# Two unread tiles of 64 and 480 bytes that shift the tile pools of an encoder layer

## The chip, the cores and the metric

The kernel runs on 1 core of one Trainium2 chip. The metric is the device time of one execution in microseconds (us), the median of several runs; lower is better. TensorE (PE in the profile) multiplies, VectorE (DVE) and ScalarE (ACT) work on elements, GpSimd (POOL) and SyncE (SP) mostly issue DMAs. A matmul has a moving operand, whose columns stream through the array, and a stationary operand of 128 by 128, which a separate weight load (PEld) puts in place beforehand. Both are read from SBUF, the on-chip memory, of which every one of the 128 partitions holds an equal stretch of bytes.

## The reference

One layer of an encoder over 256 tokens of width 2048, all in float32. Around every part stands an RMS norm before and one after:

```python
f = _swiglu(_rmsnorm(h, ffn1_pre_g[i]), ffn1_w_gate[i], ffn1_w_up[i], ffn1_w_down[i])
h = h + 0.5 * _rmsnorm(f, ffn1_post_g[i])
m = _mixer(_rmsnorm(h, mix_pre_g[i]), w_qkv[i], na_rpb[i], out_g[i], w_o[i])
h = h + _rmsnorm(m, mix_post_g[i])
f = _swiglu(_rmsnorm(h, ffn2_pre_g[i]), ffn2_w_gate[i], ffn2_w_up[i], ffn2_w_down[i])
h = h + 0.5 * _rmsnorm(f, ffn2_post_g[i])
g = jax.nn.sigmoid(_rmsnorm(h, ple_pre_g[i]) @ w_ple_gate[i])
h = h + _rmsnorm(g * (p[i] @ w_ple_proj[i]), ple_post_g[i])
```

`_swiglu(u)` is `(silu(u @ w_gate) * (u @ w_up)) @ w_down` with a hidden width of 5632. The mixer projects to q, k and v by one matrix of 2048 by 6144, attends in 16 heads of 128, and projects back by `w_o`, 2048 by 2048.

## The kernel before

**Products.** Every large product is made from two parts of each operand: a rounded high part and the low part that is left (`hid_h` and `hid_l`, `wh` and `wl`). `mac` (lines 92 to 106) issues three matmuls for each 128 rows of the inner dimension: high by high (L104), low by high (L105), high by low (L106). The activations, transposed, are the stationary operand, 128 columns of 4 bytes, which is 512 bytes in a partition. The weights are the moving operand, 512 columns, which is 2048 bytes. Weights come by DMA into `raw` or `raw_b`; `split` (lines 71 to 80) makes `wh` from them on ACT (L77) and `wl` on DVE (L78), two blocks of 128 rows at a time, into seven buffers each.

**Stages.** ffn1 and ffn2 go through the hidden width in 11 blocks of 512 columns (`swiglu`). The first block makes gate and up by plain products; the other ten use `pair_product`, which gets gate and up of both token tiles from seven products, as in Strassen's scheme, over 14 of the 16 row blocks. Of these seven, four have sums of activations as stationary operand (`sums_h`, `sums_l`, made by `token_sums`, L318 to L343; seven row blocks each, so 21 matmuls), three have the activations themselves (`u_h`, `u_l`); `rest` does the remaining row blocks, with `u_h` and `u_l` too. Between these, at the points named `fill()`, the down product of the block before is run in four pieces, each with `hid_h` and `hid_l` as stationary operand: 4 row blocks, 2 token tiles and 3 matmuls, 24 a piece. The last block's down product uses one tile `hid_2` for both parts (`hid` in the profile). The mixer's q, k and v use `u_h` and `u_l`; its output product (`mo`) uses the attention's output, again in tiles called `hid_h` and `hid_l`. The last stage's gate product (`pg`) uses `u_h` and `u_l`.

**Memory.** Pools stand one behind another: on the left side from low addresses up, in the order in which they are opened, and on the right side from the top down. A pool that is closed leaves its place to the next one. Where the tiles of the program before begin, as its allocation says, in bytes within a partition:

| tile | pool | start | remainder by 512 |
|---|---|---|---|
| `sums_h` | resid | 4096 | 0 |
| `u_h`, `u_l` (4 buffers each) | acts | 20480 and up, 36864 and up | 0 |
| `raw` (3), `wh` (7), `wl` (7) | wpool | 53248, 77824, 106496 and up | 0 |
| `y_s`, `y_g` and others | work | 135168, 137216 | 0 |
| `ssf`, `m`, `r` and others, 32 bytes each | small | 139264 to 140735 | any |
| `hid_h`, `hid_l`, `f`, `raw_b`, `sums_l` of ffn1, `hid_2`; the attention's `qT`, `kT`, `v`, `pts`; `pp`, `z` | those opened behind small | 140736 and up | 448 |
| `f`, then `sums_l` of ffn2 | f2 (right side, top at 229344) | 198624, 215008 | 480 |

The parts of `u_h`, `u_l` and `hid_h`, `hid_l` for one row block and one token tile are 512 bytes long, at steps of 1024 bytes from row block to row block and 512 from tile to tile; those of `sums_h` and `sums_l` follow each other at steps of 512 bytes.

**Order.** The framework plans the order of each engine's instructions when the program is built, so a few matmuls stand ahead of where the text of the kernel has them: the first four of the last `rest` of a `pair_product` run before the product of `a22` (L274 before L271). Engines wait for each other by semaphores that the framework puts in.

Of the kernel before, what the change touches and what calls it, by code (L numbers as in the profile page):

```python
# [8 lines left out]
F32 = mybir.dt.float32  # L9
# [6 lines left out]
P = 128  # L16
# [18 lines left out]
def encoder_layer(ctx: ExitStack, tc: tile.TileContext, a: dict, out: bass.AP):  # L35
# [13 lines left out]
    small = ctx.enter_context(tc.tile_pool(name="small", bufs=4))  # L49
# [2 lines left out]
    ps_o = ctx.enter_context(tc.tile_pool(name="ps_o", bufs=2, space=PSUM))  # L52


    ident = const.tile([P, P], F32, name="ident")
    make_identity(nc, ident)
    mhalf = const.tile([P, 16], F32, name="mhalf")
# [680 lines left out]
    f_pool = sums_pool[0] = ffn2.enter_context(tc.tile_pool(name="f2", bufs=1, side="right"))  # L738
# [46 lines left out]
        list(res)  # L785

    pool = ctx.enter_context(tc.tile_pool(name="ple", bufs=1))
    pp = []
    for n, pool_, tag in ((RQ, f_pool, "sums_l"), (NT * D // NB - RQ, pool, "pp")):
        y = pool_.tile([P, n, NB], F32, name="pp", tag=tag)  # L790
# [108 lines left out]
```

## Time and profile before

| | us |
|---|---|
| median of 3 runs (lowest, highest) | 1917.34 (1916.06, 1917.87) |
| the profiled execution's own time | 1919.31 |
| its span, first to last instruction | 1917.5 |
| PE, PEld, DVE, ACT, POOL busy | 1895.1, 1553.7, 1584.0, 1172.9, 217.5 |
| HBM read, written | 413.70 MB, 4.19 MB |

The profile is of one execution. A matmul's entry lasts from its start to a modelled end, some 390 ns for 512 columns, and the next one starts before that end. How fast TensorE really goes is therefore read from the starts: the distance from one matmul's start to the next one's. The timeline view prints starts in us with two digits; over a run of 21 or 24 matmuls the mean distance is known to about half a nanosecond.

### The profile page before, as it was taken

To read this page: it belongs to the slowest core of one execution; us is meant where nothing else is said; L and a number is where in the kernel's file an instruction comes from. 1 tells how busy PE (TensorE), PEld (TensorE's weight loads), DVE (VectorE), ACT (ScalarE), POOL (GpSimd) and SP (SyncE) were. 2 spreads that over 40 slices of the span, in tenths; PEclk is the share of its full clock that TensorE was granted. 3 is DMA by queue.
4 is the path that set the end of the run, shared out by engine and by line. 5 is a ranking of instruction groups with operands and counts; after the bars stand their busy time and mean duration, and the time that the engine had idled before them with its cause. 6 is when DMAs were issued, how large, how long until landed. Compare 5 with 4: busy or idle time off the path is not lost.

```text
span 1917.5 us, 23547 instructions
## 1 busy us (share of the span) xinstructions
PE 1895.1 (99%) x8546; PEld 1553.7 (81%) x8546; DVE 1584.0 (83%) x1825; ACT 1172.9 (61%) x1476; POOL 217.5 (11%) x189
## 2 busy tenths in 40 slices
PE   8999999999999999999999999999999999999997
PEld 6888888888888878888888888888888888888786
DVE  8889999989998986567565588899999899898954
ACT  7766666666666664554545466666666666665753
POOL 1110101010111000000000001101010111100100
PEclk9999999999999999999999999999999999999999
DMA  9879877897779567354454569789777977795562
GB/s 344 243 238 268 254 201 205 246 275 214 191 239 268 158 228 242 137 176 164 144 178 179 193 217 276 215 252 264 212 196 237 275 238 190 227 273 170 182 241 99
DMA packets 210533, 419.44 MB, mean 219 GB/s; under 512 B 8944, under 2 KB 12016, under 8 KB 209136
## 3 DMA queue, kind: packets, MB, share of 16 engines
q1 hardware_dynamic: 172304, 343.47, 50.7%
q0 software_dynamic: 38112, 74.46, 21.7%
q8 instruction: 67, 1.10, 0.2%
q14 instruction: 50, 0.41, 0.1%
HBM read 413.70 MB, written 4.19 MB: 218 GB/s over the span
## 4 chain that ended last, share of the span: by engine, by line
PE 91%; issue 5%; DVE 1%; ACT 1%; DMA 1%; POOL 0%; SPq 0%; POOLq 0%; DVEq 0%; ACTq 0%
PE pair_g L104 10%; PE pair_g L105 9%; PE pair_g L106 9%; PE down L104 8%; PE down L105 8%; PE down L106 8%; PE pair_u L105 4%; PE pair_u L104 4%; PE pair_u L106 4%; PE v L106 2%; PE v L104 2%; PE v L105 2%; PE tr L308 1%; PE q L104 1%; PE q L106 1%
## 5 line engine op out<-in xcount | busy, mean ns | idle before, releaser
L77 ACT CAST wh<-raw_b 128x1024 fp32r<-128x1024 f32 (+1 forms) x546 | 514.2, 950 | 296.2 <-PE down L105 158.2
L78 DVE TENSOR_TENSOR wl<-raw_b,wh 128x1024 fp32r<-128x1024 f32 (+1 forms) x546 | 582.3, 1097 | 75.9 <-ACT wh L77 69.0
L77 ACT CAST wh<-raw 128x1024 fp32r<-128x1024 f32 (+1 forms) x417 | 435.2, 1051 | 317.0 <-PE down L105 61.1
L78 DVE TENSOR_TENSOR wl<-raw,wh 128x1024 fp32r<-128x1024 f32 (+1 forms) x417 | 500.6, 1219 | 149.0 <-ACT wh L77 136.5
L191 POOL DMA_DIRECT2D raw_b<-in_ffn_w_up x156 | 180.3, 1197 | 1036.1 <-DVE wl L78 965.7
L105 PE MATMUL down<-wh,hid_l 128*128 128x512 f32 x640 | 251.8, 393 | 0.0
L104 PE MATMUL down<-wh,hid_h 128*128 128x512 f32 x640 | 251.1, 392 | 0.0
L106 PE MATMUL down<-wl,hid_h 128*128 128x512 f32 x640 | 248.7, 389 | 0.0
L106 PE MATMUL pair_g<-wl,u_h 128*128 128x512 f32 x502 | 196.1, 391 | 0.0
L104 PE MATMUL pair_g<-wh,u_h 128*128 128x512 f32 x502 | 195.9, 396 | 0.0
L105 PE MATMUL pair_g<-wh,u_l 128*128 128x512 f32 x502 | 195.6, 390 | 0.0
L199 DVE TENSOR_TENSOR raw_b<-raw_b 128x1024 f32<-128x1024 f32 (+1 forms) x156 | 164.4, 1096 | 0.1
L104 PEld LDWEIGHTS down<-wh,hid_h 128*128 128x128 f32 x640 | 120.2, 188 | 27.7
L106 PEld LDWEIGHTS down<-wl,hid_h 128*128 128x128 f32 x640 | 120.1, 188 | 27.0
L105 PEld LDWEIGHTS down<-wh,hid_l 128*128 128x128 f32 x640 | 120.3, 188 | 24.3
L469 DVE TENSOR_TENSOR f<-f,down 128x512 f32<-128x512 f32 x160 | 109.5, 684 | 9.3 <-PE down L106 5.2
L105 PE MATMUL pair_g<-wh,sums_l 128*128 128x512 f32 x288 | 113.8, 395 | 0.0
L104 PE MATMUL pair_g<-wh,sums_h 128*128 128x512 f32 x288 | 113.7, 395 | 0.0
L104 PEld LDWEIGHTS pair_g<-wh,u_h 128*128 128x128 f32 x502 | 94.2, 188 | 23.5 <-ACT u_s L206 3.8
L106 PE MATMUL pair_g<-wl,sums_h 128*128 128x512 f32 x288 | 112.3, 390 | 0.0
L106 PEld LDWEIGHTS pair_g<-wl,u_h 128*128 128x128 f32 x502 | 94.2, 188 | 20.6
L105 PEld LDWEIGHTS pair_g<-wh,u_l 128*128 128x128 f32 x502 | 94.3, 188 | 18.6
(227 smaller groups left out, 3028.6 us busy)
## 6 DMA issues: line engine op xcount, KB each, us to landing
raw<-in_ffn_w_down SPq DMA_DIRECT2D x88, 1024.0 KB, 8.1
raw_b<-in_ffn_w_up POOLq DMA_DIRECT2D x120, 512.0 KB, 10.3
raw<-in_w_qkv SPq DMA_DIRECT2D x48, 1024.0 KB, 5.1
raw_b<-in_ffn_w_gate SPq DMA_DIRECT2D x40, 1024.0 KB, 6.4
raw_b<-in_ffn_w_gate SPq DMA_DIRECT2D x36, 768.0 KB, 8.0
raw_b<-in_ffn_w_up SPq DMA_DIRECT2D x20, 1024.0 KB, 7.1
raw<-in_w_o SPq DMA_DIRECT2D x16, 1024.0 KB, 4.9
raw<-in_w_ple_gate SPq DMA_DIRECT2D x16, 1024.0 KB, 5.0
```

The source lines that it names most:

```text
L77: nc.scalar.copy(wh[:, :n], raw),
L78: nc.vector.tensor_tensor(wl[:, :n], raw, wh[:, :n].bitcast(F32), op=ALU.subtract),
L104: nc.tensor.matmul(acc, xh, wh, start=lead, stop=False, skip_group_check=True)
L105: nc.tensor.matmul(acc, xl, wh, start=False, stop=False, skip_group_check=True)
L106: nc.tensor.matmul(acc, xh, wl, start=False, stop=tail, skip_group_check=True)
L191: nc.gpsimd.dma_start(raw[:, k0:k1], weight_rows(w, j, c, k0, k1), accum_op=ALU.add)
L199: nc.vector.tensor_tensor(x[:, j], x[:, j], y[:, j], op=ALU.add)
L308: nc.tensor.transpose(tr[:, k], x[:, k * P : (k + 1) * P], ident)
L469: nc.vector.tensor_tensor(f_t, f_t, acc, op=ALU.add)
```

## The change

Two tiles are allocated that nothing writes or reads. The first, 16 columns of 4 bytes (64 bytes in a partition), is the first tile of the pool `small`. The second, 120 columns (480 bytes), is the third kind of tile of the pool `f2`, asked for after ffn2. No instruction is added, removed or moved in the kernel's text.

```diff
@@ -52,6 +52,7 @@
     ps_o = ctx.enter_context(tc.tile_pool(name="ps_o", bufs=2, space=PSUM))
 
 
+    small.tile([P, 16], F32, name="align", bufs=1)
     ident = const.tile([P, P], F32, name="ident")
     make_identity(nc, ident)
     mhalf = const.tile([P, 16], F32, name="mhalf")
@@ -785,6 +786,7 @@
         list(res)
 
     pool = ctx.enter_context(tc.tile_pool(name="ple", bufs=1))
+    f_pool.tile([P, 120], F32, name="align")
     pp = []
     for n, pool_, tag in ((RQ, f_pool, "sums_l"), (NT * D // NB - RQ, pool, "pp")):
         y = pool_.tile([P, n, NB], F32, name="pp", tag=tag)
```

## Prediction

> **What bounds the kernel now.** I read the page first, then the groups of instructions with shapes apart, then the timeline of TensorE.
>
> ```profile
> span 1917.5 us, 23547 instructions
> PE 1895.1 (99%) x8546; PEld 1553.7 (81%) x8546; DVE 1584.0 (83%) x1825; ACT 1172.9 (61%) x1476; POOL 217.5 (11%) x189
> PEclk9999999999999999999999999999999999999999
> PE 91%; issue 5%; DVE 1%; ACT 1%; DMA 1%; POOL 0%; SPq 0%; POOLq 0%; DVEq 0%; ACTq 0%
> ```
>
> TensorE is busy 99% of the span at full granted clock, and 91% of the chain of waits lies on it. What shortens the time must therefore shorten the distance between matmul starts. The groups give the number of matmuls by their stationary operand, the only operand of the large products that the change moves (`wh` and `wl` lie in a pool opened before `small`):
>
> ```profile
> L105 PE MATMUL down<-wh,hid_l 128*128 128x512 f32 x640 | 251.8, 393 | 0.0
> L105 PE MATMUL pair_g<-wh,sums_l 128*128 128x512 f32 x288 | 113.8, 395 | 0.0
> L105 PE MATMUL pair_u<-wh,sums_l 128*128 128x512 f32 x264 | 104.3, 395 | 0.0
> L105 PE MATMUL mo<-wh,hid_l 128*128 128x512 f32 x128 | 50.0, 391 | 0.0
> L105 PE MATMUL down<-wh,hid 128*128 128x512 f32 x64 | 25.0, 391 | 0.0
> L105 PEld LDWEIGHTS down<-wh,hid_l 128*128 128x128 f32 x640 | 120.3, 188 | 24.3
> L105 PEld LDWEIGHTS pair_g<-wh,u_l 128*128 128x128 f32 x502 | 94.3, 188 | 18.6
> ```
>
> A weight load takes 188 ns at either offset, and the matmuls' own durations are modelled, so the groups tell nothing of speed. The starts do. Here is the first matmul of each run in one stretch of ffn2, and of one run of the last stage:
>
> ```profile
> 1304.53 0.39 PE L104 MATMUL pair_u<-wh,u_h 128*128 128x512 f32 x1
> ...
> 1307.25 0.40 PE L104 MATMUL pair_u<-wh,sums_h 128*128 128x512 f32 x1
> ...
> 1312.10 0.40 PE L104 MATMUL pair_g<-wh,sums_h 128*128 128x512 f32 x1
> ...
> 1316.95 0.39 PE L104 MATMUL down<-wh,hid_h 128*128 128x512 f32 x1
> ...
> 1322.45 0.40 PE L104 MATMUL pair_g<-wh,sums_h 128*128 128x512 f32 x1
> ...
> 1863.75 0.39 PE L104 MATMUL pg<-wh,u_h 128*128 128x512 f32 x1
> ...
> 1869.19 0.39 PE L104 MATMUL pg<-wh,u_h 128*128 128x512 f32 x1
> ...
> 1874.63 0.39 PE L104 MATMUL pg<-wh,u_h 128*128 128x512 f32 x1
> ```
>
> With `u_h`, `u_l` (both at remainder 0 by 512) 12 matmuls take 2.72 us and 24 take 5.44 us twice, once for each token tile: 226.7 ns each. With `hid_h`, `hid_l` (both at 448) 24 take 5.50 us, 229.2 ns each. With `sums_h` (0) and `sums_l` (480) 21 take 4.85 us twice, 231.0 ns each. All these are back to back, with no idle time in their groups, the same clock, the same moving buffers. In ffn1, where `sums_l` is at 448:
>
> ```profile
> 279.71 0.39 PE L104 MATMUL down<-wh,hid_h 128*128 128x512 f32 x1
> ...
> 285.20 0.39 PE L104 MATMUL pair_g<-wh,sums_h 128*128 128x512 f32 x1
> ...
> 285.89 0.40 PE L104 MATMUL pair_g<-wh,sums_h 128*128 128x512 f32 x1
> ...
> 286.61 0.40 PE L104 MATMUL pair_g<-wh,sums_h 128*128 128x512 f32 x1
> ...
> 290.06 0.39 PE L104 MATMUL pair_g<-wh,u_h 128*128 128x512 f32 x1
> ```
>
> The down run takes 5.49 us, 228.8 ns a matmul, and the 21 with sums 4.86 us, 231.4 ns. Within these the first triple takes 0.69 us and the second 0.72, where `u` has 0.68 (2.72 for four). So the distance follows the low part of the stationary operand's address; a change of 32 bytes in it (448 to 480) leaves the mean and slightly changes its pattern.
>
> **The change part by part.** The first tile adds 64 bytes to `small`. Everything behind it moves from 140736 to 140800, which is 275 times 512: remainder 448 becomes 0. The second adds 480 bytes to a pool that hangs from the top, so its base goes down: `f` from 198624 to 198144 (387 times 512) and `sums_l` from 215008 to 214528 (419 times 512). No instruction, wait or DMA is added. I price each operand that becomes aligned by the distance that the aligned `u` has, 226.7 ns; this is the one step which the trace shows only for other tiles.
>
> - Sums: 3 times (288 + 264) = 1656 matmuls, now (231.0 + 231.4) / 2 = 231.2 ns: 4.5 ns less each is -7.5 us.
> - Down pieces: 3 times 640 = 1920, now (229.2 + 228.8) / 2 = 229.0: 2.3 ns each is -4.4 us.
> - The mixer's output product, 3 times 128 = 384, and the last down products, 3 times 64 = 192:
>
> ```profile
> 1060.82 0.39 PE L104 MATMUL mo<-wh,hid_h 128*128 128x512 f32 x1
> ...
> 1066.31 0.39 PE L104 MATMUL mo<-wh,hid_h 128*128 128x512 f32 x1
> ...
> 1785.69 0.39 PE L104 MATMUL down<-wh,hid 128*128 128x512 f32 x1
> ...
> 1796.68 0.39 PE L104 MATMUL down<-wh,hid 128*128 128x512 f32 x1
> ```
>
> 24 in 5.49 us and 48 in 10.99 us, so 228.8 and 229.0; 2.1 and 2.3 ns each make -0.8 and -0.4 us.
>
> What does not come through. After the third sums product (`s3`) TensorE may go on in that bank only when ACT has copied it, and four matmuls of `rest` fill that time:
>
> ```profile
> PEld pair_g L104 <- ACT u_s L206: 3.8, 18, 0.2
> L78 DVE TENSOR_TENSOR wl<-raw_b,wh 128x1024 fp32r<-128x1024 f32 x420 | 502.0, 1221 | 74.5 <-ACT wh L77 67.6
> L78 DVE TENSOR_TENSOR wl<-raw,wh 128x1024 fp32r<-128x1024 f32 x415 | 499.2, 1222 | 148.3 <-ACT wh L77 135.8 <-PE mo L106 1.5
> L77 ACT CAST wh<-raw_b 128x1024 fp32r<-128x1024 f32 x420 | 437.8, 1050 | 264.1 <-PE down L105 158.2 <-PE pair_u L105 52.7 <-PE pair_g L105 23.8
> L77 ACT CAST wh<-raw 128x1024 fp32r<-128x1024 f32 x415 | 433.9, 1053 | 316.3 <-PE down L105 61.1 <-PE pair_g L105 42.0 <-PE k L105 39.6
> 287.95 1.05 ACT L77 CAST wh<-raw 128x1024 fp32r<-128x1024 f32 x1 [0.76 <-PE pair_g L105]
> 289.04 1.23 DVE L78 TENSOR_TENSOR wl<-raw,wh 128x1024 fp32r<-128x1024 f32 x1 [0.59 <-ACT wh L77]
> 290.53 0.39 PE L106 MATMUL pair_g<-wl,u_h 128*128 128x512 f32 x1
> ```
>
> TensorE already waits there 18 times. Those four take 4 times some 5 ns less, and the wait grows by that: 18 times 0.02 is +0.4 us. The elementwise work does not change: the split of an operand at 448 (`raw_b`) takes 1221 ns on DVE and 1050 on ACT, at 0 (`raw`) 1222 and 1053, so I take zero, with bounds of 420 times 3 ns, 1.3 us, to either side, hidden as long as DVE stays ahead. The tightest place is the last three rows: ACT starts at 287.95, when TensorE has let a buffer go, DVE's `wl` ends at 290.27 and is used at 290.53, 0.26 us later. Between 287.95 and 290.53 TensorE gains 11 matmuls times 4.5 ns, 0.05 us, so the cover holds; were it gone, each 0.1 us of lateness would cost 20 blocks times 0.1, 2 us. The small products of the attention have aligned operands after the change as well. Their sum is
>
> ```profile
> L668 PE MATMUL o<-v,pts 128*128 128x128 f32 x128 | 18.4, 287 | 0.0
> L645 PE MATMUL sc<-kT_h,qT_h 128*128 128x256 f32 x32 | 10.0, 312 | 0.0
> ```
>
> 128 and three groups of 32, 224 matmuls; by the largest mean step seen above, 4.5 ns, they give between -1.0 and +1.0 us, and I take 0, the middle.
>
> Sum: -7.5 - 4.4 - 0.8 - 0.4 + 0.4 = -12.7 us. The span of 1917.5 becomes 1904.8 and the profiled execution's 1919.3 becomes 1906.6. That execution lies 2.0 us above the median of 1917.34, so the median is forecast at 1904.6 us.
>
> **The rivals.**
>
> 1. *Only one of the two groups gains.* The hid and sums tiles lie above 140000 bytes and the `u` tiles below 53248, so a high address could be the cause instead of the remainder. Against it: in both, distances vary by place in the triple (0.69 and 0.72 us), which a fixed price of a far read would not do. If only the sums gain: -7.5 + 0.4, 1910 us. If only the hid tiles gain, because `sums_h` and `sums_l` stand 200 KB apart: -5.6, 1912 us.
>
> 2. *No effect.* The distances belong to what runs beside the matmuls, DVE and ACT above all, and the stretches with `u` in the last stage have less of that. Against it: the 12 matmuls with `u` at 1304.53, between down and sums in ffn2, run at 226.7 too. Or an unread tile is dropped from the allocation, and the change does nothing. 1917.3 us either way. The Trainium skill says in "SBUF — State Buffer", section "Who interferes with whom", that PE and ACT never wait on anyone, and in its section "Operand start alignment" it asks of a start address only a multiple of the element size (for legality; it says nothing on speed). By the first of these the change would give nothing. The trace disagrees so far: 226.7, 229.0 and 231.2 ns for the same work.
>
> 3. *Slower: the sums collide at every step.* What counts may be the stationary operand's place against the moving stream, and sums aligned in both parts at steps of 512 bytes are a combination that no row shows. If each triple then ran like the worst in ffn1 (285.89 to 286.61, 0.72 us against 3 times 231.2, 0.694), 552 triples times 0.026 are +14.4 us; with the others' -5.2 the end is 1926.5 us. It is slower than before once a triple of sums exceeds 0.694 + 5.2 / 552 = 0.703 us. Against it: the `u` of the second token tile starts 512 bytes beyond that of the first, and the runs from 1863.75 and from 1869.19 both have 226.7.
>
> 4. *The second tile misses.* If it is laid elsewhere in its pool, `sums_l` of ffn2 stays at 480, half of the 7.5 us is lost, 1908.4 us.
>
> **How the numbers follow.** Chances: forecast 0.66; rival 1, 0.13; rival 4, 0.05; rival 2, 0.09; rival 3, 0.07. The forecast's own range: if aligned runs settle less well than `u` there remain some 0.6 ns on 4152 matmuls, 2.5 us, and with the bounds above, 1.0 and 1.3, about 1909; on the other side, the `u` runs that follow sums gain as well. There the run
>
> ```profile
> 97.09 0.40 PE L104 MATMUL pair_g<-wh,u_h 128*128 128x512 f32 x1
> ...
> 110.73 0.39 PE L104 MATMUL down<-wh,hid_h 128*128 128x512 f32 x1
> ```
>
> takes 13.64 us for 60, 227.3 ns, 0.6 more than elsewhere; over some 2000 matmuls with `u` in the pairs 1.2 us, with the same 1.0 and 1.3, about 1901. With rivals 1 and 4 the range is 1900 to 1915 us, which leaves out rivals 2 and 3, 0.16, and a little of the rest. A change of this kernel can be told from none beyond 0.2%, 3.8 us. Faster: forecast, rival 1 and rival 4, less a little, 0.83. Same: rival 2 and a little, 0.10. Slower: 0.07.
>
> **What would show it.** In the profile after: down runs of 24 at 5.44 us and sums runs of 21 at 4.76 us; `u` unchanged at 226.7; the same counts of instructions; DVE and ACT durations of the splits within 3 ns; the wait of PEld for ACT's `u_s` longer by some 0.02 us each. I am wrong if a run with aligned stationary operands keeps 229 or 231 ns, if a triple of sums goes beyond 0.70 us, or if matmul starts are evenly 226.7 ns and the gain turns up as waits for `wl`.

## The result and the profile after

The changed kernel takes 1904.53 us (median of 6 runs, 1902.86 to 1905.71) against 1917.52 us before on the same chip: a ratio of 0.9932 with a 95% interval of 0.9919 to 0.9944, 13.0 us faster. The forecast was 1904.6 us for the changed kernel. The profiled execution has its own time of 1905.38 us and a span of 1903.6 us.

These are the first lines of the profile after, and its chain of waits by engine:

```profile
span 1903.6 us, 23547 instructions
...
PE 1880.1 (99%) x8546; PEld 1551.1 (81%) x8546; DVE 1580.4 (83%) x1825; ACT 1174.5 (62%) x1476; POOL 217.5 (11%) x189
...
PE 91%; issue 5%; DVE 1%; ACT 1%; DMA 1%; POOL 0%; SPq 0%; POOLq 0%; DVEq 0%; ACTq 0%
```

The numbers of instructions are those of before on every engine, and so are the shares of the chain: TensorE is busy for the same share of a span that is 14 us shorter. Where the time went shows in the timeline of TensorE. Here is the first matmul of each run in the same stretch of ffn2 (all source lines stand one or two further on, since the change puts in lines; the first matmul of `mac` is now L105), and of one stretch of ffn1:

```profile
1295.10 0.39 PE L105 MATMUL pair_u<-wh,u_h 128*128 128x512 f32 x1
...
1297.82 0.39 PE L105 MATMUL pair_u<-wh,sums_h 128*128 128x512 f32 x1
...
1302.58 0.39 PE L105 MATMUL pair_g<-wh,sums_h 128*128 128x512 f32 x1
...
1307.34 0.39 PE L105 MATMUL down<-wh,hid_h 128*128 128x512 f32 x1
...
1312.78 0.39 PE L105 MATMUL pair_g<-wh,sums_h 128*128 128x512 f32 x1
...
277.78 0.39 PE L105 MATMUL down<-wh,hid_h 128*128 128x512 f32 x1
...
283.22 0.39 PE L105 MATMUL pair_g<-wh,sums_h 128*128 128x512 f32 x1
...
287.98 0.39 PE L105 MATMUL pair_g<-wh,u_h 128*128 128x512 f32 x1
```

The 12 matmuls with `u` take 2.72 us as before. Two sums runs of 21 take 4.76 us each instead of 4.85, in ffn1 4.76 instead of 4.86; the down runs of 24 take 5.44 us instead of 5.50 and 5.49. These runs now all go at the 226.7 ns that only `u` had.

### The profile page after: what moved, and what is told of

The parts are those of the page before. It is cut to its first block, busy times and chain, and to the rows that moved or that the text cites. A ratio compares the mean times of both kernels' runs of the same rounds, so it can differ in the third digit from the quotient of the medians.

```text
span 1903.6 us, 23547 instructions
## 1 busy us (share of the span) xinstructions
PE 1880.1 (99%) x8546; PEld 1551.1 (81%) x8546; DVE 1580.4 (83%) x1825; ACT 1174.5 (62%) x1476; POOL 217.5 (11%) x189
## 4 chain that ended last, share of the span: by engine, by line
PE 91%; issue 5%; DVE 1%; ACT 1%; DMA 1%; POOL 0%; SPq 0%; POOLq 0%; DVEq 0%; ACTq 0%
PE pair_g L105 10%; PE pair_g L107 9%; PE pair_g L106 9%; PE down L105 8%; PE down L107 8%; PE down L106 8%; PE pair_u L105 4%; PE pair_u L107 4%; PE pair_u L106 4%; PE v L107 2%; PE v L106 2%; PE v L105 2%; PE tr L309 1%; PE q L106 1%; PE q L105 1%
## 5 line engine op out<-in xcount | busy, mean ns | idle before, releaser
L105 PE MATMUL down<-wh,hid_h 128*128 128x512 f32 x640 | 249.0, 389 | 0.0
L105 PE MATMUL pair_g<-wh,u_h 128*128 128x512 f32 x502 | 196.1, 396 | 0.0
L105 PEld LDWEIGHTS down<-wh,hid_h 128*128 128x128 f32 x640 | 120.2, 188 | 24.9
L105 PEld LDWEIGHTS pair_g<-wh,u_h 128*128 128x128 f32 x502 | 94.2, 188 | 23.3 <-ACT u_s L207 4.2
L105 PE MATMUL pair_g<-wh,sums_h 128*128 128x512 f32 x288 | 112.0, 389 | 0.0
```

Source lines behind the costliest of these rows:

```text
L105: nc.tensor.matmul(acc, xh, wh, start=lead, stop=False, skip_group_check=True)
```

## The experiments

The theory at first: the remainder by 512 of the stationary operand's start sets the distance between matmuls. The rivals: a high address or the distance between the two parts does it, or the work beside the matmuls.

### One unread tile alone

The first kernel keeps the first tile only, the second kernel the second only.

```diff
--- after, first kernel
-    f_pool.tile([P, 120], F32, name="align")
--- after, second kernel
-    small.tile([P, 16], F32, name="align", bufs=1)
```

> Only the first unread tile (64 bytes in small). hid_h, hid_l, hid_2 and sums_l of ffn1 begin at remainder 0 by 512; sums_l of ffn2 stays at 480. By the offset theory: down runs of 24 matmuls at 5.44 us in both ffn, sums runs of 21 at 4.76 us in ffn1 and at 4.85 us in ffn2; the time is that of before less 9 us (12.7 less the half of 7.5), about 1908.5 us. Rival, that the two shifts act together and one alone is worth nothing: within 2 us of before.

> Only the second unread tile (480 bytes in the pool f2). sums_l of ffn2 begins at remainder 0, all the rest stays as before. By the offset theory: sums runs of 21 in ffn2 at 4.76 us, those of ffn1 at 4.86 us, down runs at 5.50 us; the time is that of before less 3.6 us, about 1913.8 us. Rival, that a sums run is slow because its two parts lie far apart or in different regions of the memory: it stays at 4.85 us and the time at that of before.

Measured: 1908.5 us with the first tile, ratio 0.9953 (0.9940 to 0.9965); 1913.77 us with the second, ratio 0.9975 (0.9966 to 0.9983); 1918.6 us before beside them. The first matmuls of a sums run and a down run of ffn2 tell the theories apart, here in the timeline of the first kernel and then in that of the second:

```profile
1303.72 0.40 PE L105 MATMUL pair_g<-wh,sums_h 128*128 128x512 f32 x1
...
1308.58 0.39 PE L105 MATMUL down<-wh,hid_h 128*128 128x512 f32 x1
...
1314.02 0.40 PE L105 MATMUL pair_g<-wh,sums_h 128*128 128x512 f32 x1
```

```profile
1310.22 0.39 PE L104 MATMUL pair_g<-wh,sums_h 128*128 128x512 f32 x1
...
1314.98 0.39 PE L104 MATMUL down<-wh,hid_h 128*128 128x512 f32 x1
...
1320.48 0.39 PE L104 MATMUL pair_g<-wh,sums_h 128*128 128x512 f32 x1
```

With the first tile the sums run keeps 4.86 us and the down run falls to 5.44; with the second it is the other way round, 4.76 and 5.50. In ffn1 the sums runs of 21 take 4.76 us with the first tile, which moves their `sums_l`, and 4.86 us with the second, as expected. Each tile acts alone, on the operands that it moves. The `hid` and `sums_l` tiles still lie above 140000 bytes and, within 480 bytes, as far from their other halves as before, so a high address and the distance of the parts are out as causes.

### The aligned operands shifted

```diff
--- before
+    acts.tile([P, 16], F32, name="shift", bufs=1)
+    wpool.tile([P, 112], F32, name="shift", bufs=1)
     ident = const.tile([P, P], F32, name="ident")
```

> The other way round: from the kernel before, the operands that were aligned are shifted. u_h and u_l begin at remainder 64 (64 unread bytes in front of them), 448 further unread bytes behind them keep wh and wl at remainder 0, and everything behind moves by 512 and so keeps its remainder (hid 448, sums_l 448 and 480). By the offset theory the 3690 matmuls with u lose what hid loses, 229.0 instead of 226.7 ns: 8.5 us slower than before, about 1926 us, and hid and sums runs are as before. Rival, that a high address or the work beside the matmuls makes hid slow: u stays at 226.7 ns and the time within 2 us of before.

Measured: 1939.52 us, ratio 1.0111 (1.0096 to 1.0127), 21 us slower. The direction is as the theory has it, but the price is more than twice the expected 8.5 us. The timeline of the last stage shows why, at the first matmuls of two runs of 24 with `u` at remainder 64:

```profile
1888.51 0.40 PE L106 MATMUL pg<-wh,u_h 128*128 128x512 f32 x1
...
1894.11 0.40 PE L106 MATMUL pg<-wh,u_h 128*128 128x512 f32 x1
...
1899.71 0.40 PE L106 MATMUL pg<-wh,u_h 128*128 128x512 f32 x1
```

24 take 5.60 us, 233.3 ns each instead of 226.7. Over 3690 matmuls that would be 24 us; in the two traces the distances after matmuls with `u` grew by 19.1 us in sum, since those of 300 ns and more, which contain a wait, shrank by 3.7 us. A remainder of 64 costs 6.7 ns, one of 448 cost 2.3, so it is not a matter of aligned or not, and the price needed a run of its own.

A second part of the expectation failed: the runs with `hid`, still at 448, are not as before. Here are two down runs of ffn2 with the sums run between them:

```profile
1240.34 0.40 PE L106 MATMUL down<-wh,hid_h 128*128 128x512 f32 x1
...
1245.93 0.39 PE L106 MATMUL pair_u<-wh,sums_h 128*128 128x512 f32 x1
...
1250.80 0.39 PE L106 MATMUL down<-wh,hid_h 128*128 128x512 f32 x1
...
1256.30 0.39 PE L106 MATMUL pair_u<-wh,u_h 128*128 128x512 f32 x1
```

The first takes 5.59 us, 233 ns a matmul, the second 5.50, 229 ns, with the same tiles at the same place. Of the 80 down runs 16 go at 233 ns and 64 at 229 or 230; in the kernel before all 80 go at 229 or 230. That adds 1.8 us.

### The bare matmuls at 20 places

```python
for i, o, lead, tail in steps():
    nc.tensor.matmul(o, st(sh, 448, i), mv(wh, 0, i), start=lead, stop=False)
    nc.tensor.matmul(o, st(sl, 448, i), mv(wh, 0, i), start=False, stop=False)
    nc.tensor.matmul(o, st(sh, 448, i), mv(wl, 0, i), start=False, stop=tail)
```

This is one of the 20 cases, both stationary parts at 448; each case has its own lines. `st` gives 128 columns of a stationary tile, so many bytes beyond a multiple of 512, at steps of 1024; `mv` gives 512 columns of a moving tile.

> Leaves out the whole layer: it loads one block of weights, copies it into two stationary tiles and two moving tiles that begin at multiples of 512 bytes, and runs 96 matmuls of the same three-matmul pattern for each of 20 cases, one source line triple each, with nothing beside them. Cases: both stationary parts at 0, 4, 16, 32, 64, 128, 256, 384, 448, 480 bytes beyond a multiple of 512, moving at 0; high part at 0 and low part at 32, 64, 256, 448, 480; both parts and the moving operand at 448, then stationary at 0 and moving at 448, 0 and 256, 64 and 64, 0 and 64. By the offset theory as the prediction has it: 226.7 ns at 0 and more at every other remainder, 229.0 at 448 and 231 with the parts at 0 and 480. Rival a: a coarser grid is enough, so 256 and 128 are as good as 0. Rival b: what counts is the place of the stationary operand against the moving one, so 448 with 448 and 64 with 64 are as good as 0 with 0, and stationary 0 with moving 64 is bad. Rival c: the work of other engines is needed, and all cases run at 226.7.

The timeline, at the first matmul of a case each; a case is 96 matmuls. In this order: stationary at 128, 256, 384, 448 and 480 with moving at 0, then (L158) both at 448, 0 with 448, 0 with 256, both at 64, 0 with 64.

```profile
126.64 0.39 PE L98 MATMUL acc<-wh,sh 128*128 128x512 f32 x1
...
148.95 0.39 PE L104 MATMUL acc<-wh,sh 128*128 128x512 f32 x1
...
170.71 0.40 PE L110 MATMUL acc<-wh,sh 128*128 128x512 f32 x1
...
193.03 0.40 PE L116 MATMUL acc<-wh,sh 128*128 128x512 f32 x1
...
215.43 0.40 PE L122 MATMUL acc<-wh,sh 128*128 128x512 f32 x1
...
348.56 0.39 PE L158 MATMUL acc<-wh,sh 128*128 128x512 f32 x1
...
370.33 0.40 PE L164 MATMUL acc<-wh,sh 128*128 128x512 f32 x1
...
392.73 0.39 PE L170 MATMUL acc<-wh,sh 128*128 128x512 f32 x1
...
414.53 0.39 PE L176 MATMUL acc<-wh,sh 128*128 128x512 f32 x1
...
436.33 0.39 PE L182 MATMUL acc<-wh,sh 128*128 128x512 f32 x1
```

The case at 128 takes 22.31 us (232.4 ns), at 256 21.76 (226.7), at 384 22.32, at 448 22.40 (233.3), and 480 takes 233.3 ns too. Both at 448 take 21.77 us (226.8), 0 with 448 takes 22.40, 0 with 256 and both at 64 take 21.80 (227.1, with a few slower matmuls at the start of the case), and 0 with 64, the last, takes 228.9 ns a matmul. Of those not shown here, 4 bytes take 232.4 ns and 16, 32 and 64 take 233.3; with the high part at 0 the low part at 448 or 480 takes 231.1, as in the kernel, at 64 231.2, at 32 233.3, and at 256 it takes 226.8. The first case, both parts at 0, goes at 226.7 once its first matmuls, some of which wait for the copies, are past.

So three things follow. No other engine is needed (rival c is out). A multiple of 256 bytes is as good as one of 512, but 128 is not (rival a holds for 256 alone). And what counts is the stationary operand's place against the moving one (rival b holds): 448 with 448 is as good as 0 with 0, and 0 with 448 as bad as 64 with 0. One thing did not fit: both parts at 448 with moving at 0 took 233.3 ns here and 229.0 in the kernel before.

### All operands at 64, and some at 256

Back in the full kernel, two layouts on which the new theory and the theory at first (called the title of the change below: every operand at a multiple of 512) disagree:

```diff
--- all at remainder 64, from before
+    const.tile([P, 16], F32, name="shift", bufs=1)
+    small.tile([P, 16], F32, name="align", bufs=1)
+    f_pool.tile([P, 104], F32, name="align")
--- hid and sums_l at remainder 256, from after
-    small.tile([P, 16], F32, name="align", bufs=1)
+    small.tile([P, 80], F32, name="align", bufs=1)
-    f_pool.tile([P, 120], F32, name="align")
+    f_pool.tile([P, 56], F32, name="align")
```

> Three unread tiles (64 bytes in const, 64 in small, 416 in f2): every operand of the large products, stationary and moving, begins at remainder 64 by 512, and none at a multiple of 512 or 256. New theory, from the bare matmuls (448 with 448 and 64 with 64 ran at 226.7 ns, 0 with 64 at 228.9, 64 with 0 at 233): what counts is the place of the stationary operand against the moving one. By it all runs go at 226.7 ns and the time is that of the changed kernel, 1904.5 us, within 2 us. Rival, the title of the change taken literally, that each operand must begin at a multiple of 512 bytes: u, hid and sums runs all go at 229 ns or more, 1926 us or more.

> The two tiles of the change with other sizes (320 bytes in small, 224 in f2): hid and sums_l begin at remainder 256 by 512, while u, sums_h and the moving operands stay at 0. By the theory of the relative place, whose period in the bare matmuls was 256 bytes or a divisor of it that 128 excludes (128 ran at 232.3 ns): all runs at 226.7 ns, 1904.5 us within 2 us. Rival, that in the full kernel the period is 512: hid runs stay at 229 or more and sums at 231 or more, 1917 us or more.

Measured: 1905.77 us, ratio 0.9940 (0.9928 to 0.9953), and 1903.77 us, ratio 0.9931 (0.9918 to 0.9945). Both are as fast as the changed kernel, whose interval they overlap. The sums and down runs of ffn2, first with all at 64, then with 256:

```profile
1303.62 0.39 PE L106 MATMUL pair_g<-wh,sums_h 128*128 128x512 f32 x1
...
1308.38 0.39 PE L106 MATMUL down<-wh,hid_h 128*128 128x512 f32 x1
...
1313.83 0.39 PE L106 MATMUL pair_g<-wh,sums_h 128*128 128x512 f32 x1
```

```profile
1302.51 0.39 PE L105 MATMUL pair_g<-wh,sums_h 128*128 128x512 f32 x1
...
1307.27 0.39 PE L105 MATMUL down<-wh,hid_h 128*128 128x512 f32 x1
...
1312.71 0.39 PE L105 MATMUL pair_g<-wh,sums_h 128*128 128x512 f32 x1
```

4.76 us for 21 and 5.45 or 5.44 for 24. In the first of these not one operand of the large products begins at a multiple of 512, or of 128. The full alignment is enough, but it isn't what is needed: it is enough that the starts agree with each other modulo 256.

### The same place entered from different places

> Leaves out the whole layer, as the bare matmuls before did; 96 matmuls a case. It asks why stationary 448 with moving 0 took 233.3 ns in the bare matmuls, after the case 384, but 229.0 in the kernel, where such runs follow runs with u at 0. Cases in order: 0; 448; 0; 384; 448; 0; 64; 448; 0; stationary 0 with moving 64; 0; 64; 0; 32; 0; 480; 0; 192; 0; 320; 0; 448 with 448; 0; stationary 192 with moving 448; 0. If the distance has two steady patterns and keeps the one that it enters with: 448 after 0 at 229.0, after 384 and after 64 at 233.3. If the place alone decides: 448 the same each time. By a period of 256 bytes, 192 runs as 448 does, 320 as 64 does (233.3), and 192 with moving 448 at 226.7; by a period of 512 none of the three need hold. Each case of 0 returns to 226.7.

One case differs from this text: the one announced as 448 with 448 ran stationary 448 with moving 64, which is 384 against it; it took 232.3 ns, what 384 and 128 with moving 0 take (232.3 to 232.4). The timeline at the first matmuls of the cases, in order: 448 (after 0), 0, 384, 448 (after 384), 0; then 448 (after 64, L110), 0; and then 192 (L170), 0, 320, 0.

```profile
37.14 0.39 PE L74 MATMUL acc<-wh,sh 128*128 128x512 f32 x1
...
59.12 0.39 PE L80 MATMUL acc<-wh,sh 128*128 128x512 f32 x1
...
80.88 0.40 PE L86 MATMUL acc<-wh,sh 128*128 128x512 f32 x1
...
103.20 0.40 PE L92 MATMUL acc<-wh,sh 128*128 128x512 f32 x1
...
125.59 0.39 PE L98 MATMUL acc<-wh,sh 128*128 128x512 f32 x1
...
169.78 0.40 PE L110 MATMUL acc<-wh,sh 128*128 128x512 f32 x1
...
191.76 0.40 PE L116 MATMUL acc<-wh,sh 128*128 128x512 f32 x1
...
389.86 0.39 PE L170 MATMUL acc<-wh,sh 128*128 128x512 f32 x1
...
411.83 0.39 PE L176 MATMUL acc<-wh,sh 128*128 128x512 f32 x1
...
433.59 0.40 PE L182 MATMUL acc<-wh,sh 128*128 128x512 f32 x1
...
455.99 0.39 PE L188 MATMUL acc<-wh,sh 128*128 128x512 f32 x1
```

The same place, 448 with moving 0, takes 21.98 us (229.0 ns) after 0, 22.39 (233.2) after 384 and 21.98 after 64. So this place has two steady patterns and stays for all 96 matmuls in one of them; the full kernel with `u` at 64 showed the same two for `hid`, 229 and 233 ns. After 64 the expectation, 233.3, was wrong: which pattern is taken is not simply that of the case ahead, and what decides stays open. 192 takes 21.97 us, as 448 does, and 320 takes 22.40, as 64 does: the period is 256. Stationary 192 with moving 448, which agree by 256, took 21.77 us. Each case of 0 settles at 226.7 ns; those between two others take 21.76 to 21.81 us in whole (the first, whose first matmuls take longer, takes 24.18).

## Why the prediction was right, point by point

**The bound.** TensorE's starts set the time, and they still do. The step that the trace showed only for other tiles, that an operand which becomes aligned takes the distance of `u`, held for all of them.

**The terms**, worked out from all matmul starts of the two traces (the means leave out distances of 300 ns and more, the savings are sums of all distances). Sums: 231.3 ns became 226.7 over 1656 matmuls, -7.7 us where -7.5 were forecast. Down: 229.0 became 226.7 over 1920, -4.4 as forecast. The mixer's output: -0.7 for -0.8; the last down products: -0.2 for -0.4. The small products of the attention changed by less than 0.1 us in sum for each kind of tile, where 0 was taken from a range of 1 us to either side. Matmuls with `u` gave 1.3 us that the sum did not have. The fast end of the forecast's own range had counted on 1.2, for runs that follow sums, but only 0.4 of the 1.3 lie in runs right behind sums; most lies in runs behind transposes and other small matmuls, where starts wait. With one trace of each kernel it isn't shown that the change made this part.

**What does not come through**, in the waits and groups of the profile after:

```profile
PEld pair_g L105 <- ACT u_s L207: 4.2, 18, 0.2
L107 PEld LDWEIGHTS down<-wl,hid_h 128*128 128x128 f32 x640 | 120.1, 188 | 25.2 <-DVE wl L79 0.3
L79 DVE TENSOR_TENSOR wl<-raw_b,wh 128x1024 fp32r<-128x1024 f32 x420 | 502.2, 1222 | 71.4 <-ACT wh L78 64.2 <-PE pair_u L107 0.6
L78 ACT CAST wh<-raw_b 128x1024 fp32r<-128x1024 f32 x420 | 439.9, 1055 | 255.7 <-PE down L106 153.2 <-DVE wl L79 26.6 <-PE pair_g L106 21.6
```

The wait for ACT's copy of the bank grew from 3.8 to 4.2 us over 18 times, the 0.4 that was forecast. The splits of `raw_b`, now aligned, take 1222 ns on DVE and 1055 on ACT against 1221 and 1050. On DVE that is nothing; on ACT it is 5 ns more, where a bound of 3 was given, and ACT has 1% of the chain of waits. The 5 ns repeat: `raw_b` takes 1055 in every kernel here that moves it off 448 and 1050 in every one that leaves it there. The cover held but is thinner: at the place that the prediction called the tightest, `wl` ends at 288.22 us and is used at 288.44, 0.22 us later instead of 0.26. One weight load of the down product, at 78.26 us, now waits 0.27 us for `wl`, which none did before.

**The rivals.** That only one group gains, that nothing does and that the second tile misses are refuted by the runs of 4.76 and 5.44 us and by the two kernels with one tile each. The collision of sums at every step, the slower case, did not come: each triple takes 0.68 us. Its idea, that the place against the moving stream counts, was right, though; only the combination that it feared is a good one, because the moving operands begin at multiples of 512. The rule of the Trainium skill in "SBUF — State Buffer", section "Who interferes with whom", that PE never waits on anyone, agrees with the runs in so far as no other engine was needed for the slow patterns (the bare matmuls run at up to 233.3 ns alone); but that section also calls PE's two read ports, one for the moving operand and one for weight loads, independent, and the same runs show that where the two operands start against each other costs up to 6.7 ns a matmul.

**What was not right.** The prediction let the low part of the stationary operand's own address set the distance. The runs show that its place against the moving operand does, modulo 256. The two come to the same here only because `wh` and `wl` begin at multiples of 512, and to that extent the hit was luck: with the weights at 64, the same two tiles would have left `hid` and sums at 0 against 64, which the bare matmuls ran at 228.9 ns (an estimate from that run; this layout was not run). The prediction also took a remainder of 448 to have one price; the kernel with `u` at 64 showed 6.7 ns for another remainder, and 448 itself runs at 229 or at 233 ns.

## What to carry to other kernels

Where TensorE is the bound, read the distance of its starts by operand, not the durations: a few nanoseconds between tiles that do the same work are a property of the layout, and an unread tile of 64 bytes can take them away. For 128 stationary and 512 moving columns of 4 bytes as here, begin the stationary and the moving operands at the same remainder by 256; the remainder itself made no difference in the runs with 0, 64 and 448. Before a layout is called good, look at what else a shift moves, since a shift of 64 the other way cost 21 us.

## What the runs showed of the hardware

The distance between matmuls of 512 columns with a new stationary operand each depends on the start of the stationary operand less that of the moving one, modulo 256 bytes: 226.7 ns at 0, 232.4 at 4 and at 128, 233.3 at 16, 32, 64 and 224 (480), and at 192 either 228.9 or 233.3. Which of the two a run takes is steady within it and goes with what ran ahead: the lower each time after a case of 0, the higher after 384 in both kernels of bare matmuls. What decides is open. With the high part at 0, a low part at 64, 448 or 480 makes it 231.1 or 231.2, at 32 233.3. The durations of weight loads, 188 ns before and after, and of the split on DVE, 1221 and 1222 ns, show none of this. What inside the chip makes it, whether the two reads meet at the same place of the memory or something else, none of these runs shows; that the penalty vanishes when both walk in step at the same remainder fits a meeting of the two reads, and is only argued. Other widths and types were not tried.
